# A 512-column product over the high and low part of the input in the up projections

## The chip, the cores and the metric

The kernel runs on one core of a Trainium2 chip. The time is device microseconds from start to end of one execution; lower is better. The core's engines are TensorE (PE, with PEld for its weight loads), VectorE (DVE), ScalarE (ACT), GpSimd (POOL) and SyncE (SP), which issues most of the loads.

## The reference

Three layers of a small model at batch 1, 256 tokens and width 1024, in float32: a mixer with sparse attention and a gated spatial product, a gated recurrence, and a mixture of 16 experts behind a delta-rule mixer. The first two layers each end in a feed-forward block with a short convolution over time. The change touches this block alone:

```python
def conv_ffn(x, w_up, conv_w, conv_b, w_down):      # x: 256 x 1024, w_up: 1024 x 5632, w_down: 2816 x 1024
    h = x @ w_up
    hp = jnp.pad(h, ((0, 0), (CONV_WIDTH - 1, 0), (0, 0)))            # CONV_WIDTH = 3
    y = conv_b + conv_w[2] * hp[:, 2:2 + seq]
    for j in range(2):
        y = y + conv_w[j] * hp[:, j:j + seq]
    a, b = jnp.split(y, 2, axis=-1)
    return (jax.nn.silu(a) * b) @ w_down

def first_block(...):
    for l in range(2):
        ...
        x = x + conv_ffn(rms_norm(x, ffn_norm[l]), ffn_w_up[l], ffn_conv_w[l], ffn_conv_b[l], ffn_w_down[l])
```

## The kernel before

Large products are made in three terms. A float32 matrix is cut into a high part, its rounding to the shorter format fp32r, and a low part, the float32 rest rounded in the same way. A product is then high x high + high x low + low x high, summed in PSUM. For the weights `prepare` (L165) makes the parts one unit ahead of use: ACT casts the high part (`wh`, L176), DVE subtracts to get the low part (`wl`, L177). A unit has 128 x 1024 elements. `take` (L203) hands out the next unit and first prepares the one that is three further; four pairs of buffers go round, so that the `wh` of a new unit waits until PE has used the unit four before it. The loads of the raw weights (`w`) lie on SP's queue, in five buffers.

The input of the block is normed, turned so that the model's width lies on the partitions, and cut in the same way: `xT` (L216) holds 8 slices of 128 x 256 for each part, `normT` fills them. A feed-forward block (`ffn`, L925) runs over 22 tiles of 128 of its 2816 inner columns, with a round of this loop for each j:
- `pa`, 128 inner columns x 256 tokens of the first half of the up projection, in a PSUM bank (`mm` in the rows): `formB` (L226) makes 24 products of 256 columns, three for each of the 8 slices of the width. Only the first 256 of a bank's 512 floats are used.
- the convolution of `pa` (`conv`): ACT copies it to SBUF (`yy`) scaled by the last tap and with the bias (L942), DVE adds the two shifted taps (L943, L945), each reading PSUM.
- `pb`, the second half, in the same way (`tp` in the rows), with the same `conv`.
- ACT's Silu (L977) of the first, and POOL's product with the second (L978).
- `down` of the round before: that product, cut into `gh` (ACT, L213) and `gl` (DVE, L214), times 128 rows of the down projection, 12 products of 512 columns (L961 to L963) into four PSUM banks that collect over all 22 rounds.

Two banks each serve `pa` and `pb` in turn. After each `normT` the flag `fresh` is set, and the first `formB` uses another order of the same 24 products (L233). ACT, POOL and SP take their instructions in the order of the code; in the second block and in the mixers a scheduler of the framework chooses that of DVE, and always that of PE. Every engine then works off its list in that order. In the first block (`l == 0`) some work for the next layer is added: after round 2 a cast on POOL (L596), after round 4 a softmax over two rows for the decay bounds on ACT and DVE (`lower_bounds`, L615), and copies on POOL in rounds 6 to 9.

Behind the two blocks and the mixers come the experts: 402 MB of weights through SP's queue for 16 x 32 tokens.

Of the kernel before, what the change touches and what calls it, by code (L numbers as in the profile page):

```python
# [9 lines left out]
F32R = mybir.dt.float32r  # L10
U8 = mybir.dt.uint8
AF = mybir.ActivationFunctionType
OP = mybir.AluOpType
# [5 lines left out]
S = 256  # L19
# [39 lines left out]
class Kernel:  # L59
# [20 lines left out]
    def mm(self):  # L80
        return self.psM.tile([128, 512], F32, name="mm")
# [29 lines left out]
    def plan(self):  # L111
# [23 lines left out]
        def ffn(l):  # L135
            wu, wd = I["ffn_w_up"][l], I["ffn_w_down"][l]
            pend = None
            for j0 in range(0, NJ, 2):
                va, vb = self.blk(wu, 0, 8, j0 * 128, 256), self.blk(wu, 0, 8, DFF + j0 * 128, 256)
                vd = self.blk(wd, j0, 2, 0, D)  # L140
                for jj in range(2):
                    u.extend((b, 0, 8, jj * 128, jj * 128 + 128) for b in (va, vb))
                    if pend:
# [7 lines left out]
                               ("av", rows, w, 1024), ("agv", rows, w, 3152), ("agu", rows, w, 2640), ("ao", rows, wo, 0, (0, 2)),  # L151
                               ("ao", rows, wo, 512, (0, 2)), ("ao", rows, wo, 0, (4, 6)), ("ao", rows, wo, 512, (4, 6))))
        ffn(0)
        w, wo = I["c_w_in"][0], I["c_w_out"][0]
        ordered(self.ORDER_C, (("cf", cols, w, 1024, 8), ("cq", cols, w, 0, 8), ("cia", rows, w, 2048), ("cga", rows, w, 3072),
                               ("cib", rows, w, 2560), ("cgb", rows, w, 3584), ("co", rows, wo, 0, (0, 2)),
                               ("co", rows, wo, 512, (0, 2)), ("co", rows, wo, 0, (4, 6)), ("co", rows, wo, 512, (4, 6))))
        ffn(1)
        w, wo = I["w_in_2"][0], I["w_out_2"][0]
        ordered(self.ORDER_D, (("rates", cols, w, 2048, 1), ("k", cols, w, 512, 4), ("load", cols, w, 2064, 4),  # L160
# [53 lines left out]
        self.nc.vector.tensor_tensor(l, src, h.bitcast(F32), op=OP.subtract)  # L214

    def xT(self):  # L216
        return self.chunks(self.xtp, "xT", 8)

    @staticmethod
    def chunks(pool, name, n):  # L220

        return [pool.tile([128, n, S], F32R, name=name + e) for e in "hl"]

    def formB(self, ps, x):

        wh, wl = self.take(8, 128)  # L226
        xh, xl = x
        mm = self.nc.tensor.matmul
        if self.fresh:

            for w, v, ks in ((wh, xh, range(8)), (wh, xl, range(4)), (wl, xh, range(8)), (wh, xl, range(4, 8))):
                for k in ks:
                    mm(ps, w[:, k, :], v[:, k, :], start=w is wh and v is xh and k == 0, stop=v is xl and k == 7)  # L233
            self.fresh = False
            return
        for k in range(8):
            mm(ps, wh[:, k, :], xh[:, k, :], start=k == 0, stop=False)  # L237
            mm(ps, wh[:, k, :], xl[:, k, :], start=False, stop=False)  # L238
            mm(ps, wl[:, k, :], xh[:, k, :], start=False, stop=k == 7)  # L239

    def formA(self, ps, x, k0, first, last, final=False):

        wh, wl = self.take(2, 512, final)
        xh, xl = x
        for u, t in ((0, 0), (1, 0), (0, 1), (1, 1)) if final else ((0, 0), (0, 1), (1, 0), (1, 1)):
                k = k0 + u
                a = xh[:, k, t * 128:(t + 1) * 128]
                b = xl[:, k, t * 128:(t + 1) * 128]
                self.nc.tensor.matmul(ps[t], a, wh[:, u, :], start=first and u == 0, stop=False)  # L249
                self.nc.tensor.matmul(ps[t], a, wl[:, u, :], start=False, stop=False)  # L250
                self.nc.tensor.matmul(ps[t], b, wh[:, u, :], start=False, stop=last and u == 1)
# [673 lines left out]
    def ffn(self, l):  # L925
        nc, I, sm = self.nc, self.I, self.sm
        wu, wd = I["ffn_w_up"][l], I["ffn_w_down"][l]
        with ExitStack() as st:
            wk = st.enter_context(self.tc.tile_pool(name=f"fw{l}", bufs=3))
            cw = self.cw[l]  # L930

            ps = [[self.acc() for _ in range(2)] for _ in range(2)]

            def begin(t, c):
                nc.tensor.matmul(ps[c][t], self.ident, self.half(t, c), start=True, stop=False)

            begin(0, 0)
            begin(0, 1)
            x = self.normT(between=[lambda c=c: begin(1, c) for c in range(2)])

            def conv(p, yi, ch):
                nc.scalar.activation(yi, p, AF.Identity, scale=cw[:, 2, ch:ch + 1], bias=cw[:, 3, ch:ch + 1])  # L942
                nc.vector.scalar_tensor_tensor(yi[:, 1:], p[:, :S - 1], cw[:, 1, ch:ch + 1], yi[:, 1:], op0=OP.mult,  # L943
                                               op1=OP.add)
                nc.vector.scalar_tensor_tensor(yi[:, 2:], p[:, :S - 2], cw[:, 0, ch:ch + 1], yi[:, 2:], op0=OP.mult,  # L945
                                               op1=OP.add)

            def low(yy):
                gh = wk.tile([128, S], F32R, name="gh")
                gl = wk.tile([128, S], F32R, name="gl")  # L950
                self.split_x(gh, gl, yy[:, 0, :])
                return gh, gl

            def down(j, gg):
                wh, wl = [a[:, 0, :].rearrange("p (c n) -> p c n", c=2) for a in self.take(1, D, j == NJ - 1)]
                for t in range(2):
                    a = gg[0][:, t * 128:(t + 1) * 128]
                    b = gg[1][:, t * 128:(t + 1) * 128]
                    for c in range(2):
                        o = ps[c][t]  # L960
                        nc.tensor.matmul(o, a, wh[:, c, :], start=False, stop=False)  # L961
                        nc.tensor.matmul(o, a, wl[:, c, :], start=False, stop=False)  # L962
                        nc.tensor.matmul(o, b, wh[:, c, :], start=False, stop=j == NJ - 1)  # L963

            yy = gg = None
            for j in range(NJ + 1):
                if j < NJ:
                    pa, pb = self.mm(), self.tp()
                    self.formB(pa[:, :S], x)
                if j > 0:  # L970
                    gg = low(yy)
                if j < NJ:
                    yy = wk.tile([128, 2, S], F32, name="yy")
                    conv(pa[:, :S], yy[:, 0, :], j)
                    self.formB(pb[:, :S], x)
                    conv(pb[:, :S], yy[:, 1, :], j + 22)
                    nc.scalar.activation(yy[:, 0, :], yy[:, 0, :], AF.Silu)  # L977
                    nc.gpsimd.tensor_tensor(yy[:, 0, :], yy[:, 0, :], yy[:, 1, :], op=OP.mult)  # L978
                if j > 0:
                    down(j - 1, gg)  # L980
                if l == 0 and j == 2:
                    self.load_rest()
                if l == 0 and j == 4:
                    self.lower_bounds()
                if l == 0 and 6 <= j < 10:
                    self.rest_block(j - 6)
                if j == NJ - 4:
                    gain, self.g = self.gains() if l else None, self.gains()
            self.ahead_rows = 1 - l
            for t in range(2):  # L990
                for c in range(2):
                    self.squares(t, c, ps[c][t], self.mm(), gain)
            self.ahead_rows = 2
            self.sums = ps
        self.dump(f"h{2 + 2 * l}", self.h.rearrange("p a b -> p (a b)"))
# [1128 lines left out]
```

## Time and profile before

| | |
|---|---|
| three runs | 1821.95 us median (1821.11 to 1824.43) |
| profiled execution | 1821.78 us, span of its instructions 1820.0 us |
| mean granted TensorE clock | 0.889 |
| busy in the span | PE 1439.3 us (79%), PE weight loads 940.8, DVE 688.6 (38%), ACT 521.8 (29%), POOL 286.8 (16%) |
| feed-forward stretches | 171 to 355 us and 535 to 725 us of the span |
| DMA over the span | 537.75 MB, mean 295 GB/s |

Busy times are shares of the whole span, over stages with different limits; what bounds a stage is read from that stage alone. Matmuls overlap, so the spacing from one start to the next counts for them, and not the duration of one. DVE and ACT also start an instruction somewhat before the end of the one ahead if nothing holds it.

### The profile page before, as it was taken

Reading aid. Unit: us, or ns where it says so; the run is one execution under the profiler, and the core shown is the slowest. Engines: PE = TensorE matmul, PEld = TensorE weight load, DVE = VectorE, ACT = ScalarE, POOL = GpSimd, SP = SyncE. Lnnn points to the kernel's source line nnn. Section 1 sums busy time; section 2 is a strip of 40 time slices with the busy share of each in tenths; the row PEclk is TensorE's granted clock in tenths of the full one; section 3 lists DMA queues with packets and bytes.
Section 4 is the critical chain, followed back from the end, with each engine's and each line's share of the span. In section 5 each row is a group of like instructions: output and inputs, shape, how many; then the busy total and the mean of one; then the engine's idle time right before and its main releaser. Section 6 shows DMA issues by size and latency. Waiting matters only on the chain.

```text
span 1820.0 us, 22672 instructions
## 1 busy us (share of the span) xinstructions
PE 1439.3 (79%) x9408; PEld 940.8 (52%) x9408; DVE 688.6 (38%) x1163; ACT 521.8 (29%) x918; POOL 286.8 (16%) x325
## 2 busy tenths in 40 slices
PE   8889999999899999889996567664676556865566
PEld 7868999898789998878731113110131111311111
DVE  5766777758777777786400000000000000000001
ACT  5455655554455555643210000000000000000001
POOL 6342110244520002744200000000000000000000
PEclk9989999999999999999998778787878678788878
DMA  8433655653335465323999999999999999999997
GB/s 287 148 115 132 233 179 180 188 174 109 100 124 196 164 220 174 117 71 129 417 398 427 424 424 425 427 428 427 428 429 425 425 427 426 428 427 427 426 425 290
DMA packets 134137, 537.75 MB, mean 295 GB/s; under 512 B 6455, under 2 KB 83785, under 8 KB 107922
## 3 DMA queue, kind: packets, MB, share of 16 engines
q1 hardware_dynamic: 132722, 534.15, 74.5%
q0 software_dynamic: 1152, 1.75, 0.5%
q8 instruction: 74, 1.21, 0.3%
q10 hardware_dynamic: 160, 0.41, 0.1%
q14 instruction: 29, 0.24, 0.0%
HBM read 535.21 MB, written 1.06 MB: 295 GB/s over the span
## 4 chain that ended last, share of the span: by engine, by line
DMA 46%; PE 39%; DVE 8%; POOL 2%; ACT 2%; issue 2%; SPq 0%; POOLq 0%; ACTq 0%; DVEq 0%
DMA w<-in_expert_w_gate_dram 17%; DMA w<-in_expert_w_up_dram 16%; DMA w<-in_expert_w_down_dram 12%; PE mm L237 4%; PE mm L239 4%; PE mm L238 4%; PE tp L237 2%; PE tp L238 2%; PE tp L239 2%; PE acc L961 2%; PE acc L963 2%; PE acc L962 2%; PE mm L1895 2%; DVE wl L177 2%; PE acc L249 2%
## 5 line engine op out<-in xcount | busy, mean ns | idle before, releaser
L1895 PE MATMUL mm<-w,xg 128*32 128x512 f32 x2048 | 300.8, 706 | 183.6 <-DMA w<-in_expert_w_up_dram 128.0
L177 DVE TENSOR_TENSOR wl<-w,wh 128x1024 fp32r<-128x1024 f32 x192 | 262.8, 1372 | 63.4 <-ACT wh L176 63.3
L1895 PEld LDWEIGHTS mm<-w,xg 128*32 128x32 f32 x2048 | 66.1, 123 | 407.1 <-issue 192.3
L176 ACT CAST wh<-w 128x1024 fp32r<-128x1024 f32 x238 | 247.1, 1044 | 60.4 <-PE acc L963 35.9
L1920 PE MATMUL mm<-w,gain 128*32 128x512 f32 x512 | 155.3, 772 | 98.0 <-DMA w<-in_expert_w_down_dram 91.4
L1912 DVE TENSOR_TENSOR gain<-gain,mm 128x512 f32<-128x512 f32 x16 | 11.0, 689 | 535.6 <-PE mm L1895 502.7
L237 PE MATMUL mm<-xTh,wh 128*128 128x256 f32 x712 | 205.7, 289 | 7.8 <-DVE qkv L1256 5.7
L239 PE MATMUL mm<-xTh,wl 128*128 128x256 f32 x712 | 204.6, 287 | 0.0
L238 PE MATMUL mm<-xTl,wh 128*128 128x256 f32 x712 | 204.4, 287 | 0.0
L1920 PE MATMUL tp<-w,gain 128*32 128x512 f32 (+1 forms) x544 | 154.1, 722 | 0.0
L1980 POOL TENSOR_SCALAR ss<-ss 128x1 f32<-128x1 f32 x2 | 0.8, 410 | 915.4 <-ACT acc L1978 915.3
L237 PEld LDWEIGHTS mm<-xTh,wh 128*128 128x128 f32 x712 | 138.6, 195 | 11.1 <-ACT qkv L1252 3.3
L238 PEld LDWEIGHTS mm<-xTl,wh 128*128 128x128 f32 x712 | 138.9, 195 | 2.2
L239 PEld LDWEIGHTS mm<-xTh,wl 128*128 128x128 f32 x712 | 138.8, 195 | 0.4 <-issue 0.2
L177 POOL TENSOR_TENSOR wl<-w,wh 128x1024 fp32r<-128x1024 f32 x46 | 112.2, 2447 | 107.2 <-ACT wh L176 107.2
L1920 PEld LDWEIGHTS mm<-w,gain 128*32 128x32 f32 x512 | 31.0, 133 | 140.5 <-DMA w<-in_expert_w_down_dram 71.7
L237 PE MATMUL tp<-xTh,wh 128*128 128x256 f32 x352 | 99.6, 283 | 0.0
L238 PE MATMUL tp<-xTl,wh 128*128 128x256 f32 x352 | 99.6, 283 | 0.0
L239 PE MATMUL tp<-xTh,wl 128*128 128x256 f32 x352 | 99.5, 283 | 0.0
L1914 ACT COPY gain<-tp 128x512 f32<-128x512 f32 x16 | 9.4, 586 | 287.7 <-PE tp L277 287.7
L1924 ACT COPY yv<-tp 128x512 f32<-128x512 f32 (+1 forms) x17 | 9.5, 561 | 260.5 <-PE acc L1927 257.4
L978 POOL TENSOR_TENSOR yy<-yy 128x256 f32<-128x256 f32 x44 | 32.3, 735 | 327.0 <-DVE yy L945 296.4
(523 smaller groups left out, 2436.8 us busy)
## 6 DMA issues: line engine op xcount, KB each, us to landing
w<-in_expert_w_gate_dram SPq DMA_DIRECT2D x30, 2048.0 KB, 36.7
w<-in_expert_w_up_dram SPq DMA_DIRECT2D x60, 1024.0 KB, 36.8
w<-in_expert_w_up_dram SPq DMA_DIRECT2D x13, 4096.0 KB, 39.1
w<-in_expert_w_down_dram SPq DMA_DIRECT2D x26, 2048.0 KB, 31.9
w<-in_expert_w_down_dram SPq DMA_DIRECT2D x12, 4096.0 KB, 35.5
w<-in_ffn_w_up_dram SPq DMA_DIRECT2D x44, 1024.0 KB, 5.7
w<-in_expert_w_gate_dram SPq DMA_DIRECT2D x11, 4096.0 KB, 41.6
w<-in_expert_w_gate_dram SPq DMA_DIRECT2D x24, 1024.0 KB, 36.8
```

The costliest lines, as they stand in the source:

```text
L176: nc.scalar.copy(hv, v)
L177: (on[0] if on else self.low).tensor_tensor(lv, v, hv.bitcast(F32), op=OP.subtract)
L237: mm(ps, wh[:, k, :], xh[:, k, :], start=k == 0, stop=False)
L238: mm(ps, wh[:, k, :], xl[:, k, :], start=False, stop=False)
L239: mm(ps, wl[:, k, :], xh[:, k, :], start=False, stop=k == 7)
L249: self.nc.tensor.matmul(ps[t], a, wh[:, u, :], start=first and u == 0, stop=False)
L961: nc.tensor.matmul(o, a, wh[:, c, :], start=False, stop=False)
L962: nc.tensor.matmul(o, a, wl[:, c, :], start=False, stop=False)
L963: nc.tensor.matmul(o, b, wh[:, c, :], start=False, stop=j == NJ - 1)
L978: nc.gpsimd.tensor_tensor(yy[:, 0, :], yy[:, 0, :], yy[:, 1, :], op=OP.mult)
L1895: nc.tensor.matmul(p[32 * cb:32 * cb + 32, :], x(k), w[:, cb // 2, cb % 2], start=k == 0, stop=k == 7)
L1920: nc.tensor.matmul(columns(py, c0, c1)[32 * row:32 * row + 32], h, v, start=start, stop=stop)
```

## The change

The two parts of `xT` become one tile, with the part as its first free dimension (so do the other inputs that are made by `chunks`). In the up projections, all but the first of each block, the products of `wh` with the high and with the low part of a slice become one of 2 x 256 = 512 columns, which fills a whole PSUM bank: the first half collects `wh` x high, the second `wh` x low. The product of `wl` with the high part still has 256 columns and goes to the first half. At the end ACT copies the second half to `yy`, DVE adds that to the first half in PSUM, and `conv` goes on from there.

```diff
     def xT(self):
-        return self.chunks(self.xtp, "xT", 8)
+        self.x_parts = self.xtp.tile([128, 2, 8, S], F32R, name="xT")
+        return self.x_parts[:, 0], self.x_parts[:, 1]
...
-        return [pool.tile([128, n, S], F32R, name=name + e) for e in "hl"]
+        both = pool.tile([128, 2, n, S], F32R, name=name)
+        return both[:, 0], both[:, 1]
...
+    def formB_parts(self, p, x):
+
+        if self.fresh:
+            self.formB(p[:, :S], x)
+            return False
+        wh, wl = self.take(8, 128)
+        for k in range(8):
+            self.nc.tensor.matmul(p, wh[:, k, :], self.x_parts[:, :, k, :], start=k == 0, stop=False)
+            self.nc.tensor.matmul(p[:, :S], wl[:, k, :], x[0][:, k, :], start=False, stop=k == 7)
+        return True
...
-            def conv(p, yi, ch):
-                nc.scalar.activation(yi, p, AF.Identity, scale=cw[:, 2, ch:ch + 1], bias=cw[:, 3, ch:ch + 1])
+            def conv(p, yi, ch, parts):
+                if parts:
+                    nc.scalar.copy(yi, p[:, S:])
+                    nc.vector.tensor_tensor(p[:, :S], p[:, :S], yi, op=OP.add)
+                nc.scalar.activation(yi, p[:, :S], AF.Identity, scale=cw[:, 2, ch:ch + 1], bias=cw[:, 3, ch:ch + 1])
...
                     pa, pb = self.mm(), self.tp()
-                    self.formB(pa[:, :S], x)
+                    parts = self.formB_parts(pa, x)
...
-                    conv(pa[:, :S], yy[:, 0, :], j)
-                    self.formB(pb[:, :S], x)
-                    conv(pb[:, :S], yy[:, 1, :], j + 22)
+                    conv(pa, yy[:, 0, :], j, parts)
+                    conv(pb, yy[:, 1, :], j + 22, self.formB_parts(pb, x))
```

The order of instructions on ACT in one round of the first block, from the `wh` of the next `pa` to that of the next `down`. Before (`mm` is `pa`, `tp` is `pb`, `cw` the taps; in brackets the engines whose semaphores an instruction waits for):

```order
L176 CAST wh<-w 128x1024 [waits PE_49]
L213 CAST gh<-yy 128x256 [waits Pool_49]
L942 ACTIVATE yy<-mm,cw_705 128x256 [waits PE_49]
L176 CAST wh<-w 128x1024
L942 ACTIVATE yy<-tp,cw_705 128x256 [waits PE_49]
L977 ACTIVATE yy<-yy 128x256 [waits DVE_49,Activation_49]
L176 CAST wh<-w 128x1024 [waits DMAHW4_49]
```

The same round on ACT in the changed kernel, whose line numbers are 13 to 15 higher from `conv` on:

```order
L176 CAST wh<-w 128x1024 [waits PE_49]
L213 CAST gh<-yy 128x256 [waits Pool_49]
L956 COPY yy<-mm 128x256 [waits PE_49]
L958 ACTIVATE yy<-mm,cw_703 128x256 [waits DVE_49]
L176 CAST wh<-w 128x1024
L956 COPY yy<-tp 128x256 [waits PE_49]
L958 ACTIVATE yy<-tp,cw_703 128x256 [waits DVE_49]
L992 ACTIVATE yy<-yy 128x256
L176 CAST wh<-w 128x1024 [waits DMAHW4_49]
```

The copy now waits for PE, the scaled copy behind it for DVE; each `wh` keeps its place behind a scaled copy or behind Silu.

DVE in the same round, before:

```order
L214 TENSOR_TENSOR gl<-yy,gh 128x256 [waits Activation_49]
L943 SCALAR_TENSOR_TENSOR yy<-mm,cw_705,yy 128x255 [waits Activation_49]
L945 SCALAR_TENSOR_TENSOR yy<-mm,cw_705,yy 128x254 [waits DVE_49]
L177 TENSOR_TENSOR wl<-w,wh 128x1024 [waits PE_49,Activation_49]
L943 SCALAR_TENSOR_TENSOR yy<-tp,cw_705,yy 128x255 [waits Activation_49]
L945 SCALAR_TENSOR_TENSOR yy<-tp,cw_705,yy 128x254 [waits DVE_49]
L177 TENSOR_TENSOR wl<-w,wh 128x1024 [waits DMAHW4_49,PE_49,Activation_49]
L177 TENSOR_TENSOR wl<-w,wh 128x1024 [waits DMAHW5_49,Activation_49]
```

And in the changed kernel:

```order
L214 TENSOR_TENSOR gl<-yy,gh 128x256 [waits Activation_49]
L957 TENSOR_TENSOR mm<-mm,yy 128x256 [waits Activation_49]
L959 SCALAR_TENSOR_TENSOR yy<-mm,cw_703,yy 128x255 [waits Activation_49]
L961 SCALAR_TENSOR_TENSOR yy<-mm,cw_703,yy 128x254 [waits DVE_49]
L177 TENSOR_TENSOR wl<-w,wh 128x1024 [waits Activation_49]
L957 TENSOR_TENSOR tp<-tp,yy 128x256 [waits Activation_49]
L959 SCALAR_TENSOR_TENSOR yy<-tp,cw_703,yy 128x255 [waits Activation_49]
L961 SCALAR_TENSOR_TENSOR yy<-tp,cw_703,yy 128x254 [waits DVE_49]
L177 TENSOR_TENSOR wl<-w,wh 128x1024 [waits DMAHW4_49,Activation_49]
L177 TENSOR_TENSOR wl<-w,wh 128x1024 [waits DMAHW5_49,Activation_49]
```

The add of `pa` stands between `gl` and the first shifted sum, that of `pb` between a `wl` and its first shifted sum. All else stands as before, in the second block too; outside the two blocks no engine's order differs.

## Rows read from the trace of the kernel before

**Rows 1.** Busy time by stretch: us, then each engine's busy us, PEclk, DMA share, GB/s.

```profile
171.00:355.00 184.00, 182.93 (x1278) 170.27 (x1276) 138.37 (x183) 105.66 (x162) 25.82 (x32) 1.00 0.60 199
...
535.00:725.00 190.00, 188.33 (x1323) 175.82 (x1323) 142.76 (x181) 105.70 (x163) 20.36 (x30) 1.00 0.58 191
...
920.00:1820.00 900.00, 570.13 (x3392) 163.02 (x3383) 40.72 (x88) 50.09 (x106) 1.73 (x4) 0.80 0.99 419
```

**Rows 2.** Waits of SP's queue, 700 to 960 us: us, times, longest.

```profile
SPq L87 <- DVE w L1481: 31.2, 1, 31.2
```

**Rows 3.** Timeline of PE in a round: start us, us, engine, instruction.

```profile
342.14 0.28 PE L237 MATMUL mm<-xTh,wh 128*128 128x256 f32 x1
...
345.01 0.28 PE L237 MATMUL tp<-xTh,wh 128*128 128x256 f32 x1
...
347.88 0.40 PE L961 MATMUL acc<-wh,gh 128*128 128x512 f32 x1
```

**Rows 4.** Timeline of DVE, the last round of the first block.

```profile
341.40 1.74 DVE L177 TENSOR_TENSOR wl<-w,wh 128x1024 fp32r<-128x1024 f32 x1 [0.25 <-ACT wh L176]
...
345.81 0.48 DVE L943 SCALAR_TENSOR_TENSOR yy<-mm,cw,yy 128x255 f32<-128x255 f32 x1 [0.82 <-ACT yy L942]
346.32 0.48 DVE L945 SCALAR_TENSOR_TENSOR yy<-mm,cw,yy 128x254 f32<-128x254 f32 x1
346.74 1.23 DVE L177 TENSOR_TENSOR wl<-w,wh 128x1024 fp32r<-128x1024 f32 x1
...
349.93 1.74 DVE L177 TENSOR_TENSOR wl<-w,wh 128x1024 fp32r<-128x1024 f32 x1 [0.24 <-ACT wh L176]
351.59 0.41 DVE L214 TENSOR_TENSOR gl<-yy,gh 128x256 fp32r<-128x256 f32 x1
```

**Rows 5.** Timeline of ACT in the same round.

```profile
345.21 0.56 ACT L942 ACTIVATE yy<-mm,cw 128x256 f32<-128x256 f32 x1 [1.51 <-PE mm L239]
345.67 1.03 ACT L176 CAST wh<-w 128x1024 fp32r<-128x1024 f32 x1
348.08 0.57 ACT L942 ACTIVATE yy<-tp,cw 128x256 f32<-128x256 f32 x1 [1.38 <-PE tp L239]
348.55 0.40 ACT L977 ACTIVATE yy<-yy 128x256 f32<-128x256 f32 x1
348.86 1.04 ACT L176 CAST wh<-w 128x1024 fp32r<-128x1024 f32 x1
```

**Rows 6.** Groups by line and form: count, busy us, mean ns, idle before.

```profile
L1444 DVE TENSOR_TENSOR W<-acc,block 128x256 f32<-128x256 f32 x16 | 6.5, 413 | 3.6 <-PE acc L1443 3.5
...
L1873 ACT COPY sct<-tp 128x256 f32<-128x256 f32 x16 | 6.0, 373 | 34.3 <-PE acc L1927 31.6 <-PE tp L277 2.7
```

**Rows 7.** Timelines of DVE and ACT before the first block: a handoff.

```profile
159.93 0.69 DVE L296 TENSOR_TENSOR h<-h,acc 128x512 f32<-128x512 f32 x1
...
160.66 0.60 ACT L310 ACTIVATE acc<-h 128x512 f32<-128x512 f32 x1 [0.68 <-DVE h L296]
```

**Rows 8.** Timeline of POOL in the round of rows 4.

```profile
349.85 0.73 POOL L978 TENSOR_TENSOR yy<-yy 128x256 f32<-128x256 f32 x1 [7.80 <-DVE yy L945]
```

**Rows 9.** Timelines of ACT and DVE in round 1 of the first block.

```profile
175.12 0.56 ACT L942 ACTIVATE yy<-mm,cw 128x256 f32<-128x256 f32 x1
...
176.07 0.42 DVE L214 TENSOR_TENSOR gl<-yy,gh 128x256 fp32r<-128x256 f32 x1
176.40 0.47 DVE L943 SCALAR_TENSOR_TENSOR yy<-mm,cw,yy 128x255 f32<-128x255 f32 x1
```

**Rows 10.** Side jobs in the first block: DVE, ACT, and Silu's line (ns min/median/max).

```profile
189.82 2.41 DVE L177 TENSOR_TENSOR wl<-w,wh 128x1024 fp32r<-128x1024 f32 x1 [0.31 <-ACT wh L176]
...
204.85 1.28 ACT L615 ACT_TABLE_LOAD   x1
...
L977 ACT ACT_TABLE_LOAD  x3: 1283/1283/1283, 172.2 to 540.0; - x3
```

## The prediction

> **What bounds the kernel now.** I read the busy time by stage first. In the first feed-forward stretch TensorE (PE) is busy 182.93 of 184 us at clock 1.00, DVE 138.37, ACT 105.66, POOL 25.82 and DMA 0.60; the second is alike. The last 900 us are another matter: DMA stands at 0.99 there [rows 1]. The change lies in the two feed-forward stretches, so only their length can move. What they lose or gain should reach the end almost undiluted, because the load queue starts the expert weights only when the mixer behind the second stretch frees memory: it stood 31.2 us for one such release [rows 2].
>
> Next the order of time in one round j (one `pa`, one `pb`, one `down`). PE starts `pa` at 342.14, `pb` at 345.01, `down` at 347.88 [rows 3]: 2.87 us for 24 products of 256 columns, so 0.1196 each. DVE's `wl` for the unit of `down` starts at 341.40 and, a round later, at 349.93 [rows 4], so a round is 8.53 us, and `down` has 8.53 - 5.74 = 2.79 us for 12 products of 512 columns, 0.2325 each. ACT and DVE follow PE: ACT idles 1.51 us before `pa`'s first step, ending when PE's last product has come [rows 5]. So today PE sets the round, and ACT and DVE have slack, but the slack lies in waits between two engines that each work off a list: DVE stands still for 0.82 us until ACT's scaled copy is done [rows 4], and the rest of its list stands with it.
>
> **The change on PE.** A product of weights and input goes from 24 x 0.1196 = 2.87 us to 8 x (0.2325 + 0.1196) = 2.82 us, 0.05 us less: the columns are the same, only 8 starts are saved. For 86 products (44 rounds of two, less the first of each stretch, which keeps the old form) that is 4.6 us, and a round would be 8.42 us, **if** PE went on setting it. No row shows a moving operand in two runs of 256, the new form. From above I bound it by two of 256, 0.239, no gain; from below by the bare columns at the granted 2.4 GHz, 0.213, which would save 18 us over all 86. I take 0.2325, the price of the same 512 columns. As will be seen, this term does not reach the end.
>
> **The change on ACT and DVE.** Each projection but the first gets a copy on ACT and an add on DVE, and the old scaled copy (L942) now waits for the add. Nothing else changes its order. The price of the copy is 0.37 us and of the add 0.41 us, from rows with a PSUM source and the same 256 columns [rows 6]. The add also writes PSUM, which no row of this shape shows; the upper bound is the 0.48 of the DVE step that reads the same bank [rows 4]. A handoff from DVE to ACT costs 0.04 us (a sum ends at 160.62, ACT starts at 160.66 [rows 7]); its upper bound is the 0.17 that POOL takes after a DVE step of 0.48 (POOL starts at 349.85, 1.77 after ACT's start at 348.08 [rows 5, 8], of which 0.60 + 0.52 + 0.48 are ACT's and DVE's steps).
>
> Now I go once around the new loop, starting at ACT's scaled copy of `pa` at 0, with start-to-start distances from the rows, and with PE's results taken as present:
> - DVE's two shifted sums start at 0.60 and 1.11, its `wl` for `pb` at 1.53 (345.81, 346.32, 346.74 against 345.21 [rows 4, 5]). ACT's `wh` for it starts at 0.46, takes 1.03 and is just in time.
> - A `wl` of 1.23 lets the next DVE step start some 0.08 before it ends (349.93 + 1.74 against 351.59 [rows 4]), at 2.68. Today DVE would be idle then; now **the add of `pb`** stands there, behind the `wl`: 0.41 + 0.04, and ACT's scaled copy of `pb` starts at 3.13. The ACT copy that feeds the add was done long before (ACT was through with its `wh` by 1.5), so it costs nothing here.
> - ACT: Silu 0.47 later, the next `wh` 0.31 behind it, 1.04 long [rows 5]: ready at 4.95. DVE's two sums were done earlier, so its `wl` for `down` starts at 4.99, having waited. It runs beside POOL's product and takes 1.74 instead of 1.23 [rows 4, 8], as now: next step at 6.65.
> - `wl` of the next `pa` 1.15, then `gl` 0.33 (176.07 to 176.40 [rows 9]): 8.13. **The add of the next `pa`** 0.41 + 0.04: ACT's scaled copy starts at **8.58 us**.
>
> So the loop of ACT and DVE needs 8.58 us, more than the 8.42 that PE would need and more than the 8.53 of now. The two engines do not lack throughput (DVE's share rises from 75% by two adds of 0.41 per round, to 85%); they lose it by waiting for each other in turn: while ACT's scaled copy waits for the add, the `wh` behind it waits too, and DVE's next `wl` waits for that. PE waits for `gl` in `down`.
>
> **The sum**, per stretch, up to the last `gl`, which PE's last products wait for today as well:
> - Round 1. The scaled copy of the first `pb` comes 0.37 + 0.04 + 0.41 + 0.04 = 0.86 later, and everything behind it. In round 1 ACT started the scaled copy of `pa` at 175.12; now it must wait for the add, which goes behind `gl`, where the first sum ran at 176.40 [rows 9]: 176.40 + 0.45 = 176.85, 1.73 later. Together 2.59, less the 0.05 of PE: +2.5 us.
> - Rounds 1 to 21. Today 175.12 to 345.21 = 170.1 us [rows 5, 9]; now 20 x 8.58 = 171.6: +1.5 us.
> - The end. The last `gl` starts 6.65 us after the scaled copy of `pa`; today 351.59 - 345.21 = 6.38 [rows 4, 5]: +0.3 us.
>
> That is 4.3 us, for two stretches 8.6. In the first stretch three side jobs that PE covers today lose their cover: a `wl` beside a POOL cast, 2.41 instead of 1.74 us, 0.67; the table load for the decay bounds, 1.28; and the one that brings Silu's table back, 1.28 (the second of the three at L977) [rows 10]: 3.2 us. If PE still set the round, none of the three would cost anything. Sum 11.8 us. The profiled execution took 1821.78 us (1.78 beside its span of 1820.0), 0.17 below the median of the three runs: 1821.95 + 11.8 = 1833.8, so **1834 us**.
>
> Merging the input's two tiles into one costs nothing that I find: each product waits for the same engines as before, since the parts are told apart inside the tile, and load queue and POOL keep their order.
>
> **A page against the rows.** The 0.41 of the add is a measured row with one PSUM source. The Trainium skill (VectorE: DVE Perf Modes, "The TRN2 errata") gives a VectorE instruction from PSUM a fixed 120 cycles and one per element at 0.96 GHz, so by that estimate 0.39 us for 256. By it the loop is 8.54 us and the sum some 2 us smaller, 1832; the fixed part is also what speaks against the change, since two more instructions per round pay it again.
>
> **Rivals.**
> 1. *The loop fits under PE* (0.22). It needs 0.16 us less per round, so an add with its handoff in 0.37 instead of 0.45. For it: the rows' distances are often shorter than the durations, and DVE is idle a quarter of the time. Against: every handoff in the walk waits for a whole instruction to end. Then PE's 4.6 us count, and at the end of each stretch the inserted 0.86 delays the last `gl`: 1822 - 4.6 + 1.7 = 1819 us, which no measurement here can tell from no change; only if the new product costs less than 0.2325 (its bound, 0.213, is 13 us lower) does it come out clearly faster, from 1818 down.
> 2. *The new steps are dear* (0.12): the add at 0.48 and each DVE-to-ACT handoff at 0.17. The loop is 8.58 + 2 x (0.07 + 0.13) = 8.98 us, 8 us more per stretch: 1834 + 16 = 1850 us. For it: the add reads and writes the same PSUM bank, a form without a row. It would show as a round near 9 us.
> 3. *The forecast* (0.66): 1834 us, by itself 1829 to 1841: rounds of 8.5 to 8.7 us are 3 us less and 5 us more (40 rounds), and the side jobs and the two starts may be off by 2 us.
>
> A change of 0.2% (3.6 us) is about what the measurement tells from none. The first rival gives 0.14 to "the same" and 0.08 to "faster"; the other two are slower, 0.78. The range of 8 in 10 reaches into the first rival a little and not to the far end of the second: 1823 to 1845 us.
>
> **What would show it.** Right: in the middle of a stretch the round from one scaled copy of `pa` to the next is 8.5 to 8.7 us, ACT's wait before it ends on DVE's add and no longer on PE, PE waits some 0.1 to 0.2 us per round for `gl` in `down` although its products became shorter, and the stretches end 7 and 4 us later. Wrong: rounds of 8.42 with PE busy without gaps (first rival), an add far from 0.41, a product of 512 columns far from 0.2325 us, or a `wl` that no longer meets POOL's product, which alone would take 0.5 us out of the loop and give the round back to PE.

## The result: slower by 0.8 to 1.1%

The changed kernel takes 1846.94 us in the median (1837.68 to 1848.94 over four executions, a fifth, disturbed one left out) against 1821.95 us (1821.11 to 1824.43): a ratio of 1.0113, interval 1.0094 to 1.0133. Measured again beside other runs of the kernel before (below), the ratio is 1.0082, interval 1.0065 to 1.0098, some 15 us. The forecast was 1834 us, so the direction held and the size was too small.

The profile of the changed kernel has a span of 1845.2 us. First, from its page, the chain of work that ended last, by engine:

```profile
DMA 44%; PE 22%; DVE 19%; ACT 9%; issue 4%; POOL 2%; SPq 0%; POOLq 0%; ACTq 0%; DVEq 0%
```

and the same line of the kernel before:

```profile
DMA 46%; PE 39%; DVE 8%; POOL 2%; ACT 2%; issue 2%; SPq 0%; POOLq 0%; ACTq 0%; DVEq 0%
```

DVE and ACT now carry 28% of the chain and PE 22%, where they had 10% and PE 39%. The first stretch of [rows 1], cut at the same times (the order of the engines is that of [rows 1]):

```profile
171.00:355.00 184.00, 180.04 (x930) 148.39 (x929) 147.90 (x215) 110.19 (x191) 23.45 (x26) 1.00 0.55 183
```

PE still looks busy, since the times of matmuls overlap; that it no longer leads is read from the waits. In this stretch its weight loads for `down` stand for `gl` (us, times, longest), first in the changed kernel, then before:

```profile
PEld acc L979 <- DVE gl L214: 10.4, 18, 1.9
```

```profile
PEld acc L963 <- DVE gl L214: 0.2, 1, 0.2
```

The loads run slower, 0.55 instead of 0.60; that they follow the rounds, of which fewer fall into the same time, is likely but was not tested.

How long a block lasts is read from two rows of ACT: the first cast of its normed input and the first square behind its last products. In the changed kernel:

```profile
167.10 0.59 ACT L453 CAST xT<-tp 128x512 fp32r<-128x512 f32 x1 [0.92 <-PE tp L290]
...
367.57 0.58 ACT L323 ACTIVATE mm<-acc 128x512 f32<-128x512 f32 x1 [2.05 <-PE acc L979]
...
549.57 0.59 ACT L453 CAST xT<-tp 128x512 fp32r<-128x512 f32 x1 [1.94 <-PE tp L290]
...
745.32 0.58 ACT L323 ACTIVATE mm<-acc 128x512 f32<-128x512 f32 x1 [3.77 <-DVE h L322]
```

and the same four in the kernel before:

```profile
162.30 0.59 ACT L440 CAST xTh<-tp 128x512 fp32r<-128x512 f32 x1 [0.92 <-PE tp L277]
...
352.59 0.58 ACT L310 ACTIVATE mm<-acc 128x512 f32<-128x512 f32 x1 [1.56 <-PE acc L963]
...
531.17 0.59 ACT L440 CAST xTh<-tp 128x512 fp32r<-128x512 f32 x1 [1.94 <-PE tp L277]
...
722.30 0.58 ACT L310 ACTIVATE mm<-acc 128x512 f32<-128x512 f32 x1 [3.48 <-DVE h L309]
```

The blocks grew from 190.3 and 191.1 to 200.5 and 195.8 us: 14.8 of the 25.2 us between the two spans. The other 10.4 us lie outside them, 4.8 before the first changed product is made. The experiments tell these apart.

Inside a block, one round on ACT, from one scaled copy of `pa` (L958) to the next (the bracket is idle time before an instruction and what ended it):

```profile
265.08 0.56 ACT L958 ACTIVATE yy<-mm,cw 128x256 f32<-128x256 f32 x1 [2.50 <-DVE mm L957]
265.54 1.04 ACT L176 CAST wh<-w 128x1024 fp32r<-128x1024 f32 x1
266.49 0.37 ACT L956 COPY yy<-tp 128x256 f32<-128x256 f32 x1
268.21 0.56 ACT L958 ACTIVATE yy<-tp,cw 128x256 f32<-128x256 f32 x1 [1.36 <-DVE tp L957]
...
268.99 1.99 ACT L176 CAST wh<-w 128x1024 fp32r<-128x1024 f32 x2
270.87 0.41 ACT L213 CAST gh<-yy 128x256 fp32r<-128x256 f32 x1
271.18 0.37 ACT L956 COPY yy<-mm 128x256 f32<-128x256 f32 x1
273.66 0.56 ACT L958 ACTIVATE yy<-mm,cw 128x256 f32<-128x256 f32 x1 [2.11 <-DVE mm L957]
```

and on DVE:

```profile
265.68 0.48 DVE L959 SCALAR_TENSOR_TENSOR yy<-mm,cw,yy 128x255 f32<-128x255 f32 x1 [0.63 <-ACT yy L958]
...
266.61 1.23 DVE L177 TENSOR_TENSOR wl<-w,wh 128x1024 fp32r<-128x1024 f32 x1
267.75 0.42 DVE L957 TENSOR_TENSOR tp<-tp,yy 128x256 f32<-128x256 f32 x1
268.81 0.48 DVE L959 SCALAR_TENSOR_TENSOR yy<-tp,cw,yy 128x255 f32<-128x255 f32 x1 [0.63 <-ACT yy L958]
...
270.06 2.88 DVE L177 TENSOR_TENSOR wl<-w,wh 128x1024 fp32r<-128x1024 f32 x2 [0.25 <-ACT wh L176]
272.87 0.41 DVE L214 TENSOR_TENSOR gl<-yy,gh 128x256 fp32r<-128x256 f32 x1
273.21 0.42 DVE L957 TENSOR_TENSOR mm<-mm,yy 128x256 f32<-128x256 f32 x1
```

273.66 - 265.08 = 8.58 us, where it was 8.53. In [rows 5] ACT's scaled copies waited for PE; now both wait for DVE's add, and the plain copies (L956) wait for nothing. Three times a round DVE in turn waits for ACT, 0.63 + 0.63 + 0.25 us. This is the loop.

### The profile page after: what moved, and what is told of

It reads as the page before. It is cut to its first block, busy times and chain, and to the rows that moved or that the text cites. A ratio compares the mean times of both kernels' runs of the same rounds, so it can differ in the third digit from the quotient of the medians.

```text
span 1845.2 us, 21426 instructions
## 1 busy us (share of the span) xinstructions
PE 1457.1 (79%) x8720; PEld 908.1 (49%) x8720; DVE 720.9 (39%) x1249; ACT 542.1 (29%) x1004; POOL 288.0 (16%) x325
## 4 chain that ended last, share of the span: by engine, by line
DMA 44%; PE 22%; DVE 19%; ACT 9%; issue 4%; POOL 2%; SPq 0%; POOLq 0%; ACTq 0%; DVEq 0%
DMA w<-in_expert_w_up_dram 16%; DMA w<-in_expert_w_gate_dram 15%; DMA w<-in_expert_w_down_dram 12%; DVE wl L177 9%; ACT wh L176 4%; PE mm L1910 2%; ACT yy L958 2%; PE acc L262 2%; PE acc L263 1%; PE acc L264 1%; PE mm L239 1%; PE mm L241 1%; PE mm L240 1%; PE tp L290 1%; PE tp L1122 1%
## 5 line engine op out<-in xcount | busy, mean ns | idle before, releaser
L176 ACT CAST wh<-w 128x1024 fp32r<-128x1024 f32 x238 | 243.2, 1044 | 23.9 <-PE acc L264 11.6
L250 PE MATMUL tp<-xT,wh 128*128 128x512 f32 x352 | 126.7, 399 | 0.0
L250 PE MATMUL mm<-xT,wh 128*128 128x512 f32 x336 | 120.2, 397 | 0.2 <-ACT wh L176 0.2
L239 PE MATMUL mm<-xT,wh 128*128 128x256 f32 x376 | 110.9, 295 | 8.7 <-DVE qkv L1271 6.6
L240 PE MATMUL mm<-xT,wh 128*128 128x256 f32 x376 | 109.6, 292 | 0.0
L241 PE MATMUL mm<-xT,wl 128*128 128x256 f32 x376 | 109.5, 291 | 0.0
L251 PE MATMUL tp<-xT,wl 128*128 128x256 f32 x352 | 98.9, 281 | 0.0
L251 PE MATMUL mm<-xT,wl 128*128 128x256 f32 x336 | 94.3, 281 | 0.0
L1942 PE MATMUL acc<-yv,sct 128*128 128x512 f32 (+1 forms) x132 | 69.3, 649 | 16.9 <-DVE yv L1939 11.5
L239 PEld LDWEIGHTS mm<-xT,wh 128*128 128x128 f32 x376 | 74.6, 198 | 10.2 <-ACT qkv L1267 3.3
```

Source lines behind the costliest of these rows:

```text
L176: nc.scalar.copy(hv, v)
L250: self.nc.tensor.matmul(p, wh[:, k, :], self.x_parts[:, :, k, :], start=k == 0, stop=False)
L251: self.nc.tensor.matmul(p[:, :S], wl[:, k, :], x[0][:, k, :], start=False, stop=k == 7)
L1942: nc.tensor.matmul(columns(acc[t], c0, c1), sct[:, t, :], yv, start=first, stop=last)
```

## The experiments

Twelve runs follow, in three groups of four, each beside runs of the kernel before: medians 1825.93, 1825.18 and 1823.76 us. All ratios are against those of the group. Blocks are read as above; "outside" is the rest of the span; a round is the distance between scaled copies of `pa` (plain copies where ACT makes no scaled one), as most rounds of a block show it.

| kernel | median us | ratio (interval) | blocks us | outside | round |
|---|---|---|---|---|---|
| before (profile shown first) | | | 190.3 + 191.1 = 381.4 | 1438.6 | 8.53 |
| changed (profile above) | 1846.94 | 1.0113 (1.0094, 1.0133) | 200.5 + 195.8 = 396.2 | 1449.0 | 8.58 |
| again | 1841.68 | 1.0082 (1.0065, 1.0098) | 201.3 + 195.7 = 396.9 | 1445.6 | 8.58 |
| merge_only | 1826.06 | 1.0003 (0.9992, 1.0014) | 190.3 + 191.3 = 381.6 | 1446.3 | 8.53 |
| no_wait | 1842.64 | 1.0092 (1.0076, 1.0109) | 200.9 + 195.3 = 396.3 | 1444.0 | 8.56 |
| fold_alone | 1842.41 | 1.0093 (1.0078, 1.0108) | 201.3 + 195.7 = 397.0 | 1444.0 | 8.58 |
| no_fold | 1822.35 | 0.9975 (0.9961, 0.9988) | 187.6 + 188.4 = 376.0 | 1444.5 | 8.40 |
| add_late | 1822.67 | 0.9987 (0.9977, 0.9997) | 189.0 + 189.0 = 378.0 | 1441.3 | 8.40 |
| early_wh | 1825.12 | 1.0005 (0.9992, 1.0018) | 190.8 + 189.6 = 380.4 | 1442.9 | 8.15, then 8.40 |
| taps_on_dve | 1824.25 | 0.9996 (0.9984, 1.0009) | 189.1 + 189.2 = 378.3 | 1442.9 | 8.40 |
| mul_on_dve | 1828.27 | 1.0023 (1.0012, 1.0035) | 191.9 + 189.4 = 381.3 | 1446.3 | 8.25 |
| early_mul | 1819.91 | 0.9982 (0.9968, 0.9996) | 188.7 + 188.6 = 377.3 | 1437.8 | 7.88, then 8.40 |
| side_moved | 1841.03 | 1.0087 (1.0068, 1.0106) | 196.5 + 195.7 = 392.2 | 1447.8 | 8.58 |
| taps_again | 1823.89 | 1.0002 (0.9990, 1.0014) | 189.1 + 189.2 = 378.3 | 1444.3 | 8.40 |

**The changed kernel once more**, without an edit.

> The changed kernel a second time. The first profile of it is 25.2 us longer than that of before: 14.8 us inside the two feed-forward blocks (from their norm to their last product) and 10.1 us outside them, 4.8 of these before the first changed product. Theory (loop of ACT and DVE): the 14.8 us come again within 1 us, with rounds of 8.6 to 9.0 us. On the 10.1 us two readings part: if they are scatter between executions, a second profile shows another figure there (0 to 6 us) at the same inside part; if the merged input tile causes them, they come again, with the first block's norm near 167 us of the span and not near 162.

The blocks came again within 0.7 us (396.9), the outside part did not: 1445.6 against 1449.0. The first norm stood at 163.75 us, not at 167.1.

**The merge alone.** Only the input's tiles are merged:

```diff
     def formB_parts(self, p, x):
-        if self.fresh:
-            self.formB(p[:, :S], x)
-            return False
+        self.formB(p[:, :S], x)
+        return False
```

> The merge of the two input tiles alone: all products in the old form, 24 of 256 columns, no copy, no add. The prediction's step says that merging costs nothing: 1822 us within 2, and the blocks as long as before (190.3 and 191.1 us from norm to last product). Rival: the merge costs the 10.1 us that the changed kernel shows outside the two blocks: 1827 to 1832 us, at unchanged blocks.

The merge costs nothing: ratio 1.0003, blocks 381.6. Its outside part is 1446.3, 7.7 above the profile of before at the same products in the same places. So most of the 10 us outside the blocks is scatter between executions; what makes it wasn't looked for.

**Work without the wait, first try:**

```diff
-                    nc.scalar.copy(yi, p[:, S:])
-                    nc.vector.tensor_tensor(p[:, :S], p[:, :S], yi, op=OP.add)
+                    q = wk.tile([128, S], F32, name="q")
+                    nc.scalar.copy(q, p[:, S:])
+                    nc.vector.tensor_tensor(q, p[:, :S], q, op=OP.add)
```

> The changed products, with the copy and the add still done on ACT and DVE, but into a tile of their own that nobody reads, so that the scaled copy doesn't wait for the add (the high x low term is thereby left out of the sum). Theory (the wait closes a loop between ACT and DVE): PE sets the round again at 8.4 us, the blocks come out 2 us shorter each than before, 15 to 19 us less than the changed kernel: 1818 to 1830 us, the upper part if the merge costs. Rival (the additional work on ACT and DVE itself is what costs): rounds stay at 8.6 us or more and the time within 5 us of the changed kernel, 1838 to 1848.

1842.64 us, as the rival said, but the edit did not do what it was meant to. ACT's timeline of this run,

```profile
266.02 0.56 ACT L959 ACTIVATE yy<-mm,cw 128x256 f32<-128x256 f32 x1 [2.49 <-DVE q L958]
```

shows the scaled copy still waiting for the add; it starts 0.04 after the add ends (265.57 + 0.41), as in the changed kernel. The scaled copy doesn't need the add's result, and neither writes the bank that both read: the program keeps the order that the code gives to two readers of one bank. The run says nothing on work against wait.

**The copy and the wait alone, with the old products:**

```diff
-            self.nc.tensor.matmul(p, wh[:, k, :], self.x_parts[:, :, k, :], start=k == 0, stop=False)
+            self.nc.tensor.matmul(p[:, :S], wh[:, k, :], x[0][:, k, :], start=k == 0, stop=False)
+            self.nc.tensor.matmul(p[:, :S], wh[:, k, :], x[1][:, k, :], start=False, stop=False)
...
-                    nc.scalar.copy(yi, p[:, S:])
-                    nc.vector.tensor_tensor(p[:, :S], p[:, :S], yi, op=OP.add)
+                    nc.scalar.copy(yi, p[:, :S])
+                    nc.vector.tensor_tensor(p[:, :S], p[:, :S], yi, op=OP.max)
```

> The copy, the add's place and the wait alone, with the old products of 256 columns: ACT copies the first half of the bank, DVE takes the maximum of it and its copy in PSUM, which leaves the sum as it was, and the scaled copy waits for that. Theory (loop): as slow as the changed kernel within 3 us, 1838 to 1848, rounds of 8.6 to 9.0 us, although PE's products are the old ones. Rival (the product of 512 columns in two runs is itself dear or disturbs PE): back near 1822 to 1827 us.

1842.41 us, blocks 397.0: the whole loss, without one product of 512 columns in the up projections. ACT's waits in its first block (us, times, longest):

```profile
ACT yy L959 <- DVE mm L958: 45.9, 21, 3.7
ACT yy L959 <- DVE tp L958: 29.2, 22, 1.4
```

In the changed kernel they are the same to 0.1 us:

```profile
ACT yy L958 <- DVE mm L957: 45.8, 21, 3.7
ACT yy L958 <- DVE tp L957: 29.2, 22, 1.4
```

So what PE saves per product does not reach the end at all, as the prediction said.

**The product alone:**

```diff
-                if parts:
-                    nc.scalar.copy(yi, p[:, S:])
-                    nc.vector.tensor_tensor(p[:, :S], p[:, :S], yi, op=OP.add)
```

> The product of 512 columns alone: the copy and the add are left out, and the scaled copy and the shifted sums read the first half of the bank alone, as before the change (the high x low term of the up projections is left out). Both theories expect PE to set the round: 8 pairs at 0.350 us and 12 x 0.2325 give 8.4 us, the two blocks together 375 to 378 us from norm to last product, against 381.4 of before and 396 to 397 of the changed kernel: 4 to 6 us faster than before. If the blocks stay above 385 us, the product itself is dear.

Blocks 376.0 us, 5.4 less than before, and rounds of 8.40. PE's timeline:

```profile
300.21 0.40 PE L250 MATMUL tp<-xT,wh 128*128 128x512 f32 x1
300.44 0.28 PE L251 MATMUL tp<-xT,wl 128*128 128x256 f32 x1
300.56 0.39 PE L250 MATMUL tp<-xT,wh 128*128 128x512 f32 x1
```

A pair takes 0.35 us, 0.23 and 0.12, so the moving operand in two runs of 256 costs no more than one of 512. This is the most that the product can give here, by the ratio 0.25%.

**Work without the wait, second try:** the scaled copy ahead of the add.

```diff
                 if parts:
-                    nc.scalar.copy(yi, p[:, S:])
-                    nc.vector.tensor_tensor(p[:, :S], p[:, :S], yi, op=OP.add)
+                    q = wk.tile([128, S], F32, name="q")
+                    nc.scalar.copy(q, p[:, S:])
                 nc.scalar.activation(yi, p[:, :S], AF.Identity, scale=cw[:, 2, ch:ch + 1], bias=cw[:, 3, ch:ch + 1])
+                if parts:
+                    nc.vector.tensor_tensor(q, p[:, :S], q, op=OP.add)
```

> The run with the add into a tile of its own still had the wait: the program orders the reads of a bank by two engines, so ACT's scaled copy went on waiting for DVE's add before it. Here the scaled copy stands ahead of the add, so that ACT waits for PE alone, while copy, add and all other work on ACT and DVE remain (the add's result is read by nobody, so the high x low term is left out). Theory (the wait closes a loop): PE sets the round at 8.4 us, the two blocks together 376 to 381 us. Rival (the work of copy and add itself costs): the blocks stay at 390 us or more. In between, 381 to 390, both count.

Blocks 378.0 us and rounds of 8.40, with every copy and add still done. ACT's timeline has its waits for PE back:

```profile
302.36 0.37 ACT L957 COPY q<-mm 128x256 f32<-128x256 f32 x1 [1.23 <-PE mm L251]
302.63 0.57 ACT L958 ACTIVATE yy<-mm,cw 128x256 f32<-128x256 f32 x1
```

So the order of waits is the cause. The additional work alone costs 2 us (378.0 against 376.0 of the product alone), of the 20 that separate the changed kernel from that.

**One `wh` earlier**, all outputs made. `prepare` is cut in two, ACT's cast (`begin_unit`) and DVE's subtraction:

```diff
                     nc.scalar.copy(yi, p[:, S:])
+                    if early:
+                        self.begin_unit()
                     nc.vector.tensor_tensor(p[:, :S], p[:, :S], yi, op=OP.add)
...
-                    conv(pb, yy[:, 1, :], j + 22, self.formB_parts(pb, x))
+                    conv(pb, yy[:, 1, :], j + 22, self.formB_parts(pb, x), j > 0)
```

> The changed kernel with one step moved: ACT's wh for the unit of down stands right behind the copy of pb, ahead of the scaled copy that waits for the add; wl keeps its place on DVE. Work, add and wait are those of the changed kernel, the outputs complete. Theory (loop): DVE's wl for down no longer waits for the wh behind Silu, 0.3 us leave the loop of 8.58 us, it fits under PE's 8.4, and the blocks shrink from 396.5 to 378 to 385 us, the time by 11 to 18 us. Rival (work alone, or the order of the shifted sums): the blocks stay above 392 us.

Blocks 380.4, 16 us less than the changed kernel, by moving one instruction. On ACT the `wh` at 271.92 now fills the wait for the add:

```profile
270.25 0.57 ACT L968 ACTIVATE yy<-mm,cw 128x256 f32<-128x256 f32 x1 [0.56 <-DVE mm L967]
...
271.92 1.06 ACT L185 CAST wh<-w 128x1024 fp32r<-128x1024 f32 x1
...
278.40 0.56 ACT L968 ACTIVATE yy<-mm,cw 128x256 f32<-128x256 f32 x1 [0.56 <-DVE mm L967]
```

The loop takes 278.40 - 270.25 = 8.15 us; in each such round the block makes good 0.25 of its late start, until PE leads at 8.40.

**The fold without a way back to ACT**, all outputs made, and once more for the interval:

```diff
-                    nc.scalar.copy(yi, p[:, S:])
-                    nc.vector.tensor_tensor(p[:, :S], p[:, :S], yi, op=OP.add)
-                nc.scalar.activation(yi, p[:, :S], AF.Identity, scale=cw[:, 2, ch:ch + 1], bias=cw[:, 3, ch:ch + 1])
+                    q = wk.tile([128, S], F32, name="q")
+                    nc.scalar.copy(q, p[:, S:])
+                    nc.vector.tensor_tensor(q, p[:, :S], q, op=OP.add)
+                    p = q
+                    nc.vector.tensor_scalar(yi, q, cw[:, 2, ch:ch + 1], cw[:, 3, ch:ch + 1], op0=OP.mult, op1=OP.add)
```

> The changed products with another fold, outputs complete: the add writes a tile in SBUF, DVE itself makes the scaled copy with the bias from it, and the two shifted sums read it too; ACT makes only the plain copy. DVE has as many steps as before and one more per projection than the changed kernel, ACT one less, and no engine goes to another and back inside a projection. Theory (loop): PE sets the round, the blocks take 376 to 381 us together, 2 to 5 us less than before the change. Rival (DVE's work is what costs): with more work on DVE the blocks are longer than the changed kernel's 396.5 us.

> The fold with the scaled copy on DVE a second time, on another chip perhaps: blocks of 378.3 us again within 0.5, and a ratio to before between 0.997 and 1.001; its 3 us gain in the blocks is at the edge of what the scatter outside the blocks lets the total show.

DVE has one step more per projection than in the changed kernel, and yet the blocks take 378.3 us, both times: 18 less than the changed kernel, 3.1 less than before. The totals (0.9996 and 1.0002) don't tell those 3 us from nothing.

**The product with the second half on DVE**, all outputs made:

```diff
-                    nc.gpsimd.tensor_tensor(yy[:, 0, :], yy[:, 0, :], yy[:, 1, :], op=OP.mult)
+                    nc.vector.tensor_tensor(yy[:, 0, :], yy[:, 0, :], yy[:, 1, :], op=OP.mult)
```

> The changed kernel with one instruction on another engine: the product of Silu's result with the second half goes from POOL to DVE, outputs complete. DVE gets 0.41 us more per round, into its wait of 0.3 us for the wh of down; the wl that ran beside POOL should take 1.23 instead of 1.75 us. By the walk round the loop: 8.58 - 0.5 + 0.1 = 8.2 us, below PE's 8.4, so that PE sets the round and the two blocks take 378 to 386 us together, 1824 to 1832 us. Rival (DVE's work counts, not the order of waits and the meeting with POOL): rounds of 8.6 to 9.0 us, blocks at 397 us or more.

DVE's timeline:

```profile
300.52 2.35 DVE L177 TENSOR_TENSOR wl<-w,wh 128x1024 fp32r<-128x1024 f32 x2
```

DVE now has the product too, 0.43 us a round, and yet the loop takes 8.25 us and not 8.58, because two `wl` take 2.35 instead of 2.88. The blocks take 381.3. It is the 0.5 us that the prediction named as what would give the round back to PE. But at 0.15 under PE's 8.40 the loop makes good the late start only by the 17th round of the second block, and in the first block not at all, so PE did not set the rounds as this run's expectation had it.

**Both moves**, the `wh` of early_wh and the product of mul_on_dve, by the two diffs above.

> Both moves at once, wh of down's unit ahead of the scaled copy of pb and the product on DVE, outputs complete. If each takes a wait of its own out of the loop it is near 8.0 us, and the side jobs of the first block are covered sooner: blocks 377 to 380 us, 1 to 4 us under before. If the two take out the same wait, no better than the better of them alone.

The loop falls to 7.88 us, the blocks to 377.3. This is the one version with all outputs whose interval lies below 1: 0.9982 (0.9968 to 0.9996), 3.9 us, about the 4.1 by which its blocks are shorter than before. It is the best of several versions and the interval ends close to 1, so the gain is small and not beyond doubt.

**The side jobs** behind the last round of the first block:

```diff
-                if l == 0 and j == 2:
-                    self.load_rest()
-                if l == 0 and j == 4:
-                    self.lower_bounds()
-                if l == 0 and 6 <= j < 10:
-                    self.rest_block(j - 6)
...
+            if l == 0:
+                self.load_rest()
+                self.lower_bounds()
+                for i in range(4):
+                    self.rest_block(i)
```

> The changed kernel with the side jobs of the first block (POOL's cast, the decay bounds with their table load, POOL's four copies) moved behind its last round, outputs complete. The prediction gave them 3.2 us. The rows of the changed kernel's rounds give 1.56 + 1.28 + 0.9 + 4 x 0.39 = 5.3 us above 8.58. Theory by the rows: the first block shrinks by 5 to 5.5 us to 195.2 to 196.2, the length of the second. Rival by the prediction's term: it shrinks by 3.2 only, to 197.5 to 198. The total isn't forecast, since the jobs now stand in the path of the next stage.

All rounds from the third on are 8.55 to 8.59. Counted from the first scaled copy of `pa` to the last, the rounds take 180.2 us instead of 185.6: the jobs cost 5.4, as the rows said. The block shrank by 4.0 only (4.8 against the second profile), because the jobs now meet the last round. Its `gl`, by DVE's timeline, stands beside POOL's cast (357.96 to 360.06):

```profile
358.34 2.00 DVE L214 TENSOR_TENSOR gl<-yy,gh 128x256 fp32r<-128x256 f32 x1
```

That is 1.6 us more than the 0.41 of other rounds, with PE waiting for it. The total is that of the changed kernel (1.0087 against 1.0082): what the block gained does not show in it.

## Why the prediction was right, and where too small

**Right: the loop.** The walk from rows of before gave 8.58 us, and the rounds are 8.58. Its stations hold to 0.01 us in the rows shown above: counted from ACT's scaled copy at 265.08, the add of `pb` starts at 2.67 (2.68 in the walk), the `wl` for `down` at 4.98 (4.99), `gl` at 7.79 (7.80) and the next add at 8.13 (8.13). The prices held: the copy 0.37, the add 0.42 (0.41 in the sum). The add in the changed kernel, with two forms for the two banks:

```profile
L957 DVE TENSOR_TENSOR tp<-tp,yy x44: 424/426/432, 176.9 to 738.2; 128x256 f32<-128x256 f32 x44
L957 DVE TENSOR_TENSOR mm<-mm,yy x42: 417/420/428, 182.1 to 735.0; 128x256 f32<-128x256 f32 x42
```

The 0.39 us that was worked out from the Trainium skill (VectorE: DVE Perf Modes, "The TRN2 errata") is 0.03 short of it; the row there has results that go to SBUF, and the add writes PSUM. The page's estimate of 8.54 us for the loop fell with it. The handoff is 0.04 (267.75 + 0.42 to 268.21).

**Right: the terms for the start and the rounds.** Without side jobs (side_moved) the first block's rounds take 180.2 us, before they took 176.2 (169.02 to 345.21, from the first scaled copy to the last): 4.0, where 2.5 + 1.5 had been forecast. In the second block they are 4.1 longer.

**Right: PE's gain doesn't reach the end, and the merge is free.** fold_alone and merge_only show the two. The rivals fell: the loop doesn't fit under PE (8.58 against 8.40), and nowhere but beside POOL's jobs is it near 8.98.

**Too small: the side jobs.** This is the term of the sum that was mis-sized, the step "three side jobs that PE covers today lose their cover ... 3.2 us". They cost 5.4, by side_moved. Rows of the changed kernel, first DVE,

```profile
196.09 4.45 DVE L177 TENSOR_TENSOR wl<-w,wh 128x1024 fp32r<-128x1024 f32 x2 [0.24 <-ACT wh L176]
...
262.76 1.60 DVE L177 TENSOR_TENSOR wl<-w,wh 128x1024 fp32r<-128x1024 f32 x1
```

then POOL:

```profile
197.36 2.10 POOL L609 CAST levels<-w 128x1920 uint8<-128x1920 f32 x1
...
261.82 1.47 POOL L619 COPY levels<-levels 32x480 uint8<-32x480 uint8 x1
```

The pair of `wl` at 196.09 took 4.45 instead of 2.88: 1.57, where I had 0.67. I had set the 2.41 of [rows 10] against a `wl` that meets POOL's product (1.74), while its place is that of one that meets nothing (1.23); and with the rounds in ACT's and DVE's hands it came earlier into the cast, and stood longer. The four copies of rounds 6 to 9, which I had not counted, make four rounds of 8.97 us, 0.39 each, 1.6 together.

The rounds of the two table loads take 9.86 and 9.49, so 1.28 and 0.9 more, where I had 2.56 for both. That the first comes to just the 1.28 of its load is luck. The rows of that round, ACT first, then DVE,

```profile
216.21 1.03 ACT L176 CAST wh<-w 128x1024 fp32r<-128x1024 f32 x1
...
216.48 0.15 DVE L629 TENSOR_TENSOR lm<-lb 128x8 f32<-128x8 f32 x1
...
217.60 1.23 DVE L177 TENSOR_TENSOR wl<-w,wh 128x1024 fp32r<-128x1024 f32 x1
```

show that the `wh` behind the load is done at 217.24, while the small DVE steps of the decay bounds hold the `wl` until 217.60. They cost the round 1.12 us there, and two more of them behind the `wl` 0.15; the load alone would have cost some 0.8 (217.24 + 0.04 - 216.48), by estimate. The second load delays Silu, so that POOL's product is over (226.00) before the next pair of `wl` starts (226.10): the pair takes 2.36 instead of 2.88, which gives part of the load's time back.

The Trainium skill (SBUF — State Buffer, "SBUF: two separate sides") says that DVE and POOL take a shared pair of ports under a lock, and that the one that comes second stands still until the other's whole instruction is over. The rows of the cast and the copies agree: the `wl` of 262.76 ends 1.07 behind the end of POOL's copy (261.82 + 1.47), and the second of 196.09 ends 1.08 behind that of the cast (197.36 + 2.10), not much less than the 1.23 that a `wl` takes alone.

**Too small: the end**, 0.3 us forecast, 0.8 and 0.5 measured as what remains of the blocks' 10.2 and 4.6 behind the rounds' 9.4 and 4.1. The last `gl` itself came as forecast, 6.63 us after the scaled copy of `pa` in the first block (366.08 - 359.45), where 6.65 stood against 6.38 of before. What the sum took as unchanged are the products behind it. Here the changed kernel waits for `gh` with PE idle, and TensorE's clock falls. Its PE timeline,

```profile
365.57 0.50 PE L977 MATMUL acc<-wh,gh 128*128 128x512 f32 x1 [3.85 <-ACT gh L213]
...
368.19 0.63 PE L979 MATMUL acc<-wh,gl 128*128 128x512 f32 x1
368.61 0.63 PE L977 MATMUL acc<-wh,gh 128*128 128x512 f32 x1
```

and its stretches around it, granted clock third from the right:

```profile
360.00:366.00 6.00, 2.15 (x10) 1.45 (x9) 5.01 (x7) 3.43 (x7) 0.72 (x1) 1.00 0.52 176
367.00:370.00 3.00, 3.00 (x8) 1.88 (x6) 1.42 (x3) 1.98 (x6) 1.05 (x4) 0.50 0.88 252
```

After an idle time of 3.85 us the last products of the block, from the sixth on, ran at 1.2 GHz, 0.42 us apart instead of 0.23. Before, PE waited 0.24 us at the same place and its last products stayed 0.23 apart:

```profile
351.08 0.50 PE L961 MATMUL acc<-wh,gh 128*128 128x512 f32 x1 [0.24 <-ACT gh L213]
...
353.32 0.39 PE L961 MATMUL acc<-wh,gh 128*128 128x512 f32 x1
353.55 0.40 PE L962 MATMUL acc<-wl,gh 128*128 128x512 f32 x1
```

In the second block of the changed kernel the last products are 0.42 to 0.43 apart too. At the end of the first block it is so in all six profiles in which PE stood 3.7 to 3.9 us there, and in none of the eight with 0.2 to 2.1 us. At the end of the second block, however, two others show it too (merge_only and early_wh), with waits about as short as in the kernel before.

**Not in the forecast: the rest of the first measurement.** 1846.94 lies 2 us above the range of 1823 to 1845, the second median of 1841.68 within it. The blocks account for 14.8 to 15.5 us, about what the second measurement shows (1841.68 - 1825.93 = 15.8). The span outside the blocks scatters from 1437.8 to 1449.0 us over the fourteen profiles, and the first pair of profiles fell near its two ends. It averages 1446.1 us over the five profiles with rounds of 8.56 or 8.58 us and 1442.8 over the nine others. Of these 3.3 us, 1.7 lie ahead of the first norm, where the change has done nothing yet; between the blocks the five are not longer (178.7 against 178.9), and behind the second block they are by 1.8. Whether that part is more than scatter stays open.

## What to carry to other kernels

An added step of 0.4 us on an engine that is idle a quarter of the time can still slow a kernel, if it makes one engine's list wait for the other's in the middle of a round: add up the whole way round, start to start, and compare it with the round of the engine that leads. Then look for an instruction that can stand in the wait: one cast moved ahead of it took out 16 us, more than the change's saving on PE could give here (5.4 in the blocks). And once the lead passes to another engine, every side job of that engine loses its cover at the same moment, so count them all, with the times at which they will then fall.

## What the runs showed of the hardware

A matmul whose 512 moving columns come in two runs of 256 takes the 0.23 us of one in a single run. DVE's `gl` of 128 x 256 took 2.00 us instead of 0.41 beside a cast on POOL. And the last products of the changed kernel's first block ran at half the clock (granted 0.50) after PE had idled 3.85 us, 0.42 us apart instead of 0.23, so that this wait at the end of a stage cost more than its length.
